# Moving the value products of two mixers to the steps of later heads' scores and transposes

## The chip, the cores and the metric

The kernel runs on one core of one Trainium2 chip. The time is device microseconds of one execution; a run's figure is the median of several executions. TensorE (PE) multiplies, VectorE (DVE) and ScalarE (ACT) work element by element and empty PSUM, GpSimd (POOL) and SyncE (SP) mostly issue transfers. PSUM is the memory of eight banks into which TensorE writes.

## The reference

One block of a streaming encoder, on 256 frames of width 2048, all in float32: a half-step SwiGLU feed-forward, two token mixers side by side, a second feed-forward and a norm. Only the mixers are touched here.

```python
att = chunked_band_attention(q_a, k_a, v_a, rel_bias)      # 8 heads of 128
#   scores = q k^T * 128**-0.5 + bias, masked; p = softmax(scores); out = p v
ret = chunkwise_retention(rotary(q_r), rotary(k_r), v_r)   # 8 heads of 128
#   scores = q k^T * decay; out = scores v; out = out * rsqrt(mean(out * out) + EPS)
ret = silu(g_r) * ret
merged = sigmoid(gate_a) * (att @ w_out_att) + sigmoid(gate_r) * (ret @ w_out_ret)
x = x + merged @ w_out
```

## The kernel before

Nearly all work is matrix products with weights that stream in once. The program is a hand-written list of **steps**. A standard step takes one piece of weights, 256 rows by 512 columns, multiplies it with both halves of the frames and adds into two PSUM banks. For accuracy each float32 number is split into a high part (`hi`, ScalarE, line 126) and a low part (`lo`, VectorE, line 127), and three products of those are added (lines 137, 138 and 140): twelve products of 512 columns in a standard step.

`run` writes the steps out in order. For step c it first prepares weights up to step c+3 (`prep_upto`: a cast on ScalarE and a subtraction on VectorE; four `hi`/`lo` buffers exist, so the cast for step c+3 needs the buffer that step c-1 has read). Then it writes out everything that is due at step c (the table `due`, filled by `later(n, fn)`), and then the products of step c. Each engine does its own instructions in this order, so what is due at step c stands on TensorE ahead of the twelve products of c, and on ScalarE and VectorE behind the split for step c+3.

The mixers' own small products have no steps. They are due at steps of the projections that run meanwhile, and they are plain float32 products, not split ones. Steps are counted here from m, the first step of the second projection of retention's values: m to m+7 is that projection, m+8 to m+23 retention's first queries and keys (heads 0 to 3), m+24 to m+39 its second (heads 4 to 7), m+40 to m+55 the four blocks of attention's output product (`woa`), and from m+56 the four blocks of retention's (`wor`). The second feed-forward comes after them.

Attention, head h, opened at m+4+4h, in stages that the tuple at line 948 places:

- `scores` (tile `as`, +0): two products into a side bank; VectorE then adds the bias and takes the maximum.
- `powers` (+1) and `shares` (+2): exponentials on ScalarE, divisions on VectorE.
- `transposes` (tile `apt`, +4): three transposes into a side bank, which ScalarE copies out (line 937).
- `values` (tile `av`, +6): two products into a side bank; ScalarE casts the result to `atth` (line 376), VectorE subtracts to `attl` (line 377).

So at step m+4+4h stand the transposes of head h-1 and the scores of head h, and two steps later, alone or with a transpose of retention's queries and keys (`qr`, `kr`), the values of head h-1.

Retention, half b (four heads), opened `RET_WAIT[b]` steps after its keys are complete, so at m+37 and m+44: head i has its scores (tile `rs`) at +2i and its values (tiles `ro`) at +2i+3. The four heads of a half share two output banks, and `finish`, at +9, squares them, takes the root on GpSimd and scales them on VectorE into `rg` (line 999). Three steps later `ret.put` transposes `rg` (tile `retp`) and splits it into `reth` and `retl`, which `wor` multiplies. Its block 0 uses heads 4 to 7 from its third step, m+58.

All of `as`, `apt`, `av`, `rs`, `retp`, the transposes of `qr` and `kr`, and `gps` (the turn of a norm's gains, due at m+52, copied out by VectorE at line 293) write **side** tiles, and there are two side banks:

```python
def side_tile(name):
    return psum.tile([P, NB], F32, tag="side", name=name, bufs=2)
```

A tile takes a bank that was given back, and its first product waits until the last reader of that bank is done.

Of the kernel before, what the change touches and what calls it, by code (L numbers as in the profile page):

```python
# [37 lines left out]
HALF_K = D // P // 2  # L38
LEAD = 12
MIX_LEAD = 8  # L40
RET_WAIT = (14, 5)
HELD = 6

SHARE = (0.85,) * 4 + (1.0,) * 4 + (0.8,) + (0.4,) * 3 + (0.15,) * 4
# [28 lines left out]
def block_kernel(ctx: ExitStack, tc: tile.TileContext, x, g1, w1g, w1u, w1d, gm, w_in, rel, woa, wor, wo,  # L73
# [12 lines left out]
    def act_tile(dt, name):  # L86
        return apool.tile([P, 4, SEQ], dt, tag="act", name=name)

    def acc_tile(name, tag="acc"):
        return psum.tile([P, NB], F32, tag=tag, name=name, bufs=3)  # L90

    def side_tile(name):
        return psum.tile([P, NB], F32, tag="side", name=name, bufs=2)

    def tmp_tile(name, tag="t", bufs=None):
        return tmp.tile([P, NB], F32, tag=tag, name=name, bufs=bufs)
# [9 lines left out]
    def later(n, fn):  # L106
        due.setdefault(state["step"] + n, []).append(fn)
# [261 lines left out]
    def rsqrt(dst, ssum, n, width):  # L369

        v = small.tile([P, width], F32, tag="v", name="v")
        nc.vector.tensor_scalar(v, ssum, 1.0 / n, EPS, op0=ALU.mult, op1=ALU.add)
        nc.gpsimd.tensor_tensor(dst, v, mhalf[:, :width], op=ALU.pow)

    def split_out(ps, hi, lo):
        nc.scalar.copy(hi, ps)
        nc.vector.tensor_sub(lo, ps, hi.bitcast(F32))
# [513 lines left out]
    def attention(h):  # L891
        b, i = h // 4, h % 4
        hs = slice(i * HD, (i + 1) * HD)
        sm = {}

        def scores():
            q, k = tposed["qa", b], tposed["ka", b]
            ps = side_tile(f"as{h}")
            nc.tensor.matmul(ps[:, 0:SEQ], q[:, i, P:SEQ], k[:, i, :], start=True, stop=True)
            nc.tensor.matmul(ps[:, SEQ : SEQ + P], q[:, i, 0:P], k[:, i, 0:P], start=True, stop=True)  # L900
            room = act_tile(F32, f"p{h}").rearrange("p a q -> p (a q)")
            s = room[:, : 3 * P].rearrange("p (j k) -> p j k", j=3)
            sm["room"] = room
            p3 = ps[:, : 3 * P].rearrange("p (j k) -> p j k", j=3)

            for j, bj in ((0, 1), (1, 0), (2, 0)):
                nc.vector.scalar_tensor_tensor(
                    s[:, j, :], p3[:, j, :], scale, table["bias", b][:, i, bj * P : (bj + 1) * P], op0=ALU.mult, op1=ALU.add
                )
            m = small.tile([P, NT], F32, tag="m", name="m")  # L910
            tot = small.tile([P, NT], F32, tag="l", name="l")
            for t, js in ((1, slice(0, 2)), (0, slice(2, 3))):
                nc.vector.reduce_max(m[:, t : t + 1], s[:, js, :], axis=AX.XY)
            nc.vector.tensor_scalar_mul(m, m, -1.0)
            sm["p"], sm["m"], sm["tot"] = s, m, tot


        def powers():
            s, m, tot = sm["p"], sm["m"], sm["tot"]
            for t, js in ((1, slice(0, 2)), (0, slice(2, 3))):  # L920
                nc.scalar.activation(
                    s[:, js, :], s[:, js, :], AF.Exp, bias=m[:, t : t + 1], accum_out=tot[:, t : t + 1]
                )

        def shares():
            s, tot = sm["p"], sm["tot"]
            nc.vector.reciprocal(tot, tot)
            for t, js in ((1, slice(0, 2)), (0, slice(2, 3))):
                nc.vector.tensor_scalar_mul(s[:, js, :], s[:, js, :], tot[:, t : t + 1])

        def transposes():
            ps = side_tile(f"apt{h}")

            for j, c in ((2, 0), (0, 1), (1, 2)):
                nc.tensor.transpose(ps[:, c * P : (c + 1) * P], sm["p"][:, j, :], id_sb)
            pt = sm.pop("room")[:, 3 * P : 6 * P]
            nc.scalar.copy(pt, ps[:, : 3 * P])
            sm["pt"] = pt

        def values():  # L940
            v = nat["va", b]
            ps = side_tile(f"av{h}")
            nc.tensor.matmul(ps[:, :SEQ], v[:, 0, hs], sm["pt"][:, :SEQ], start=True, stop=False)
            nc.tensor.matmul(ps[:, P:SEQ], v[:, 1, hs], sm["pt"][:, SEQ:], start=False, stop=True)
            hi, lo = att.alloc(b)
            split_out(ps[:, :SEQ], hi[:, i, :], lo[:, i, :])

        return (0, scores), (1, powers), (2, shares), (4, transposes), (6, values)

    def all_attention():  # L950
        for h in range(HEADS):
            for s, stage in attention(h):
                later(2 + 4 * h + s, stage)

    def retention(b):

        wait = RET_WAIT[b]
        outs = {}

        def head(i):  # L960
            h = 4 * b + i
            hs = slice(i * HD, (i + 1) * HD)
            sm = {}

            def scores():
                q, k = tposed["qr", b], tposed["kr", b]
                ps = side_tile(f"rs{h}")
                nc.tensor.matmul(ps[:, 0:SEQ], k[:, i, 0:P], q[:, i, :], start=True, stop=True)
                nc.tensor.matmul(ps[:, SEQ : SEQ + P], k[:, i, P:SEQ], q[:, i, P:SEQ], start=True, stop=True)
                s = act_tile(F32, f"rp{h}").rearrange("p a q -> p (a q)")[:, : 3 * P]  # L970
                nc.vector.tensor_mul(s[:, :SEQ], ps[:, :SEQ], table["decay", b][:, i, :])
                nc.vector.tensor_mul(s[:, SEQ:], ps[:, SEQ : SEQ + P], table["decay", b][:, i, 0:P])
                sm["s"] = s

            def values():
                if i == 0:
                    for t in range(NT):
                        outs[t] = acc_tile(f"ro{b}{t}", ("acc", "z")[t])
                v = nat["vr", b]
                s = sm["s"]  # L980
                nc.tensor.matmul(outs[0][:, hs], s[:, 0:P], v[:, 0, hs], start=True, stop=True)
                nc.tensor.matmul(outs[1][:, hs], s[:, P:SEQ], v[:, 0, hs], start=True, stop=False)
                nc.tensor.matmul(outs[1][:, hs], s[:, SEQ:], v[:, 1, hs], start=False, stop=True)

            return scores, values

        def finish():
            srcs = []
            for t in range(NT):
                sq = tmp_tile(f"rsq{b}{t}", "gate", 2)  # L990
                nc.scalar.activation(sq, outs[t], AF.Square)
                ms = small.tile([P, 4], F32, tag="ms", name="ms")
                nc.vector.reduce_sum(ms, sq.rearrange("p (h d) -> p h d", h=4), axis=AX.X)
                rs = small.tile([P, 4], F32, tag="rs", name="rs")
                rsqrt(rs, ms, HD, 4)
                o = tmp_tile(f"rg{b}{t}", "qk", 4)
                for i in range(4):
                    hs = slice(i * HD, (i + 1) * HD)
                    nc.vector.scalar_tensor_tensor(
                        o[:, hs], outs[t][:, hs], rs[:, i : i + 1], nat["gr", b][:, t, hs], op0=ALU.mult, op1=ALU.mult  # L1000
                    )
                srcs.append(o)
            later(3, lambda: [ret.put(b, t, srcs[t]) for t in range(NT)])

        for i in range(4):
            for s, stage in enumerate(head(i)):
                later(wait + 2 * i + 3 * s, stage)
        later(wait + 2 * 4 + 1, finish)

    w_in0 = w_in[0]  # L1010

# [37 lines left out]
    for b in range(2):  # L1049
        add([proj(QR + b * NB, ret_qk_done("qr", b)), proj(KR + b * NB, ret_qk_done("kr", b, lambda b=b: retention(b)))])  # L1050
# [207 lines left out]
```

## Time and profile before

| what | before |
|---|---|
| median of 3 runs | 2061.78 us (2060.89 to 2064.99) |
| the profiled execution | 2063.49 us |
| its span, first to last instruction | 2061.4 us |
| TensorE busy | 2045.3 us, 99% of the span |
| VectorE busy | 1754.4 us, 85% |
| ScalarE busy | 1402.9 us, 68% |
| granted TensorE clock, mean | 0.999 of 2.4 GHz |
| HBM read | 462.65 MB |

The profile is of one execution and its times are microseconds from its first instruction. The profiled execution took 2.1 us more than its span and 1.71 us more than the median.

### The profile page before, as it was taken

The numbers are of one execution on the slowest core, as the hardware profiler recorded it, in microseconds if no ns is written. First come the engines' busy times: TensorE is split into PE (matmuls) and PEld (weight loads), VectorE is DVE, ScalarE is ACT, GpSimd is POOL, SyncE is SP. The second block draws the span as 40 slices with busy tenths as digits, with TensorE's granted clock in tenths as the row PEclk, the third lists the DMA queues.
The fourth block names the chain that finished last, engine by engine and source line by source line (L and its number), as shares of the span: only waits on it lengthen the run. The fifth ranks groups of instructions, "written<-read, shape, count | busy, mean of one in ns | idle before, by whom it ended". The sixth has DMA issues, their size and how long they took to land.

```text
span 2061.4 us, 26148 instructions
## 1 busy us (share of the span) xinstructions
PE 2045.3 (99%) x9256; PEld 1691.9 (82%) x9256; DVE 1754.4 (85%) x1824; ACT 1402.9 (68%) x1732; POOL 273.3 (13%) x322
## 2 busy tenths in 40 slices
PE   9999999999999999999999999999999999999998
PEld 7788888888888888888888888888888878888886
DVE  7998899899997799899966667568989988998986
ACT  7677667777777767776665434556776677677785
POOL 1111211122111110122100000010122012110200
PEclk9999999999999999999999999999999999999999
DMA  8776876788678777788775645575787668876873
GB/s 308 207 225 230 269 227 207 239 264 258 191 231 258 240 205 251 258 284 260 227 267 175 223 143 187 187 245 170 235 273 234 200 224 273 240 206 233 281 215 133
DMA packets 219315, 473.28 MB, mean 230 GB/s; under 512 B 14816, under 2 KB 15568, under 8 KB 219184
## 3 DMA queue, kind: packets, MB, share of 16 engines
q1 hardware_dynamic: 161088, 309.89, 44.7%
q0 software_dynamic: 54752, 155.88, 27.9%
q10 hardware_dynamic: 3344, 5.84, 0.8%
q8 instruction: 72, 1.18, 0.2%
q14 instruction: 59, 0.48, 0.1%
HBM read 462.65 MB, written 8.91 MB: 229 GB/s over the span
## 4 chain that ended last, share of the span: by engine, by line
PE 93%; DVE 3%; DMA 2%; ACT 1%; issue 1%; SPq 0%; DVEq 0%; POOLq 0%; POOL 0%; ACTq 0%
PE acc L140 17%; PE acc L137 17%; PE acc L138 17%; DMA raw<-in_ffn_w_down_dram 2%; DVE lo L127 1%; ACT hi L126 0%; PE z684a L140 0%; PE z380a L137 0%; PE z953a L138 0%; PE z684a L138 0%; PE z418a L137 0%; PE z723a L138 0%; PE z380a L140 0%; PE z281a L138 0%; PE z723a L137 0%
## 5 line engine op out<-in xcount | busy, mean ns | idle before, releaser
L127 DVE TENSOR_TENSOR lo<-raw,hi 128x1024 fp32r<-128x1024 f32 x399 | 487.1, 1224 | 179.1 <-ACT hi L126 174.3
L126 ACT CAST hi<-raw 128x1024 fp32r<-128x1024 f32 x399 | 417.7, 1050 | 226.8 <-PE acc L138 143.7
L775 ACT ACTIVATE acc<-xall 128x512 f32<-128x512 f32 x96 | 57.5, 599 | 8.0 <-DVE f1g L742 3.6
L778 ACT ACTIVATE xall<-acc 128x512 f32<-128x512 f32 x96 | 56.6, 589 | 9.2 <-PE acc L140 7.4
L137 PE MATMUL acc<-hi,mgh 128*128 128x512 f32 x128 | 50.2, 392 | 0.0
L138 PE MATMUL acc<-hi,mgl 128*128 128x512 f32 x128 | 49.9, 390 | 0.0
L137 PE MATMUL acc<-hi,nma01h 128*128 128x512 f32 x96 | 38.7, 403 | 0.0
L137 PE MATMUL acc<-hi,nma00h 128*128 128x512 f32 x96 | 38.6, 402 | 0.0
L138 PE MATMUL acc<-hi,nma00l 128*128 128x512 f32 x96 | 37.5, 391 | 0.0
L137 PE MATMUL acc<-hi,nma10h 128*128 128x512 f32 x96 | 37.5, 391 | 0.0
L138 PE MATMUL acc<-hi,nma01l 128*128 128x512 f32 x96 | 37.5, 390 | 0.0
L138 PE MATMUL acc<-hi,nma11l 128*128 128x512 f32 x96 | 37.5, 390 | 0.0
L137 PE MATMUL acc<-hi,nma11h 128*128 128x512 f32 x96 | 37.4, 390 | 0.0
L138 PE MATMUL acc<-hi,nma10l 128*128 128x512 f32 x96 | 37.4, 390 | 0.0
L140 PE MATMUL acc<-lo,mgh 128*128 128x512 f32 x128 | 35.6, 390 | 0.0
L140 PE MATMUL acc<-lo,nma01h 128*128 128x512 f32 x96 | 29.6, 390 | 0.0
L140 PE MATMUL acc<-lo,nma00h 128*128 128x512 f32 x96 | 29.6, 390 | 0.0
L140 PE MATMUL acc<-lo,nma11h 128*128 128x512 f32 x96 | 29.6, 390 | 0.0
L140 PE MATMUL acc<-lo,nma10h 128*128 128x512 f32 x96 | 29.6, 390 | 0.0
L140 PEld LDWEIGHTS acc<-lo,mgh 128*128 128x128 f32 x128 | 24.0, 188 | 5.0
L137 PEld LDWEIGHTS acc<-hi,mgh 128*128 128x128 f32 x128 | 24.1, 188 | 4.9
L138 PEld LDWEIGHTS acc<-hi,mgl 128*128 128x128 f32 x128 | 24.1, 188 | 4.8
(6130 smaller groups left out, 6933.7 us busy)
## 6 DMA issues: line engine op xcount, KB each, us to landing
raw<-in_ffn_w_down_dram SPq DMA_DIRECT2D x176, 512.0 KB, 6.1
raw<-in_w_in_dram SPq DMA_DIRECT2D x96, 512.0 KB, 4.7
raw<-in_ffn_w_up_dram SPq DMA_DIRECT2D x32, 512.0 KB, 10.2
raw<-in_w_out_dram SPq DMA_DIRECT2D x32, 512.0 KB, 4.0
raw<-in_ffn_w_gate_dram SPq DMA_DIRECT2D x31, 512.0 KB, 5.9
raw<-in_w_out_att_dram SPq DMA_DIRECT2D x16, 512.0 KB, 4.3
raw<-in_w_out_ret_dram SPq DMA_DIRECT2D x16, 512.0 KB, 4.0
z380x<-in_w_in_dram POOLq DMA_DIRECT2D x8, 512.0 KB, 7.4
```

The source lines that it names most:

```text
L126: nc.scalar.copy(hi, raw)
L127: nc.vector.tensor_sub(lo, raw, hi.bitcast(F32))
L137: nc.tensor.matmul(acc, ahi, whi, start=first, stop=False, **more)
L138: nc.tensor.matmul(acc, alo, whi, start=False, stop=False, **more)
L140: nc.tensor.matmul(acc, ahi, wlo, start=False, stop=last, **more)
L775: nc.scalar.activation(acc, xs[t][:, cols], AF.Copy, scale=2.0)
L778: nc.scalar.activation(xs[t][:, cols], acc, AF.Copy, scale=0.5)
```

## The change

Three numbers move. Attention's values are due eight steps after their scores in place of six, so that values of h-2, transposes of h-1 and scores of h now share a step, in this order. Retention's values are due four steps after their scores in place of three, which makes them share a step with the scores of head i+2. Its first half opens two steps later, and `finish` comes one step later relative to its half.

```diff
-RET_WAIT = (14, 5)
+RET_WAIT = (16, 5)
...
-        return (0, scores), (1, powers), (2, shares), (4, transposes), (6, values)
+        return (0, scores), (1, powers), (2, shares), (4, transposes), (8, values)
...
             for s, stage in enumerate(head(i)):
-                later(wait + 2 * i + 3 * s, stage)
-        later(wait + 2 * 4 + 1, finish)
+                later(wait + 2 * i + 4 * s, stage)
+        later(wait + 2 * 4 + 2, finish)
```

In steps:

| what | before | after |
|---|---|---|
| attention, scores of h / transposes of h | m+4+4h / m+8+4h | the same |
| attention, values of h | m+10+4h | m+12+4h |
| retention, scores of heads 0 to 3 | m+37, 39, 41, 43 | m+39, 41, 43, 45 |
| retention, values of heads 0 to 3 | m+40, 42, 44, 46 | m+43, 45, 47, 49 |
| retention, finish / put of the first half | m+46 / m+49 | m+49 / m+52 |
| retention, scores of heads 4 to 7 | m+44, 46, 48, 50 | the same |
| retention, values of heads 4 to 7 | m+47, 49, 51, 53 | m+48, 50, 52, 54 |
| retention, finish / put of the second half | m+53 / m+56 | m+54 / m+57 |

The order in which TensorE stands to do its work around step m+16, as a difference (- before, + after). `av1` is the value product of head 1, `apt2` the transposes of head 2, `as3` the scores of head 3; a bracket names the engine's counter on which the instruction waits.

```order
-L943 MATMUL av1_9328<-p1_9178,va0_8071 128x256 [waits Activation_49]
-L944 MATMUL av1_9328<-p1_9178,va0_8071 128x128
...
+L943 MATMUL av1_9376<-p1_9178,va0_8071 128x256 [waits DVE_49]
+L944 MATMUL av1_9376<-p1_9178,va0_8071 128x128
 L935 MATMUL apt2_9381<-id_sb_78,p2_9281 128x128 [waits DVE_49,PE_49]
 L935 MATMUL apt2_9381<-id_sb_78,p2_9281 128x128 x2
-L899 MATMUL as3_9386<-ka0T_7123,qa0T_6271 128x256 [waits PE_49]
+L899 MATMUL as3_9386<-ka0T_7123,qa0T_6271 128x256 [waits Activation_49]
 L900 MATMUL as3_9386<-ka0T_7123,qa0T_6271 128x128
```

The two products of `av1` went down two steps, to just ahead of `apt2`, and the scores `as3` behind them now wait on ScalarE's counter, where before they waited on TensorE's own.

ScalarE at the same place, before. `hi` are casts of weights, `qr00` and `qr01` empty the two banks of retention's query projection (line 869), `p2<-apt2` copies the transposes out.

```order
L376 CAST atth0_9230<-av1_9328 128x256 [waits PE_49]
L126 CAST hi586_9348<-raw586_9225 128x1024 [waits DMAHW6_49,PE_49,Activation_49]
L869 ACTIVATE qr00_9366<-acc64_0_9187,nmrstd_91 128x512 [waits PE_49]
L869 ACTIVATE qr01_9368<-acc64_1_9188,nmrstd_91 128x512 [waits PE_49]
L126 CAST hi587_9371<-raw587_9253 128x1024 [waits DMAHW7_49,Activation_49]
L937 COPY p2_9281<-apt2_9381 128x384 [waits PE_49]
```

And after:

```order
L126 CAST hi586_9343<-raw586_9225 128x1024 [waits DMAHW6_49,PE_49,Activation_49]
L869 ACTIVATE qr00_9361<-acc64_0_9187,nmrstd_91 128x512 [waits PE_49]
L869 ACTIVATE qr01_9363<-acc64_1_9188,nmrstd_91 128x512 [waits PE_49]
L126 CAST hi587_9366<-raw587_9246 128x1024 [waits DMAHW7_49,Activation_49]
L376 CAST atth0_9269<-av1_9376 128x256 [waits PE_49]
L937 COPY p2_9281<-apt2_9381 128x384 [waits PE_49]
```

The cast `atth` of the value product moved from ahead of `hi586` to between `hi587` and the copy of `apt2`.

TensorE at step m+52, before: the values of head 6 at m+51 (`ro`, from `rp6`), the gains' turn `gps2` at m+52, the values of head 7 at m+53.

```order
L981 MATMUL ro10_10323<-vr1_9161,rp6_10351 128x128
L982 MATMUL ro11_10324<-vr1_9161,rp6_10351 128x128
L983 MATMUL ro11_10324<-vr1_9161,rp6_10351 128x128
...
L292 MATMUL gps2_10458<-id_sb_78,grows2_10217 128x16 [waits DMASW7_49,DVE_49]
...
L981 MATMUL ro10_10323<-vr1_9161,rp7_10414 128x128 [waits DVE_49]
```

And after, where `retp00` and `retp01` are the transposes of retention's first half:

```order
L981 MATMUL ro10_10314<-vr1_9161,rp6_10322 128x128 [waits DVE_49]
L982 MATMUL ro11_10315<-vr1_9161,rp6_10322 128x128
L983 MATMUL ro11_10315<-vr1_9161,rp6_10322 128x128 [waits DVE_49]
L292 MATMUL gps2_10442<-id_sb_78,grows2_10208 128x16 [waits DMASW7_49]
L382 MATMUL retp00_10447<-id_sb_78,rg00_10356 128x128 [waits DVE_49]
L382 MATMUL retp00_10447<-id_sb_78,rg00_10356 128x128 x3
L382 MATMUL retp01_10454<-id_sb_78,rg01_10369 128x128 [waits DVE_49]
L382 MATMUL retp01_10454<-id_sb_78,rg01_10369 128x128 x3
```

The values of head 6 and both transposes of the first half came to the step of `gps2`: three side tiles in one step, of which the third, `retp01`, waits on VectorE. The rows of VectorE at that place, after, from the end of `finish` of the first half to the split of its first transposes:

```order
L999 SCALAR_TENSOR_TENSOR rg01_10369<-ro01_10172,rs_10365,gr0_9372 128x128 x3
L127 TENSOR_TENSOR lo621_10387<-raw621_10238,hi621_10386 128x1024 [waits DMAHW1_49,PE_49,Activation_49]
L971 TENSOR_TENSOR rp7_10398<-rs7_10395,decay1_9507 128x256 [waits PE_49]
L972 TENSOR_TENSOR rp7_10398<-rs7_10395,decay1_9507 128x128
L127 TENSOR_TENSOR lo622_10414<-raw622_10265,hi622_10413 128x1024 [waits DMAHW2_49,PE_49,Activation_49]
L1072 TENSOR_TENSOR siga2_10078<-acc70_0_10325,siga2_10078 128x512 [waits DMASW5_49,PE_49]
L1072 TENSOR_TENSOR siga2_10078<-acc70_1_10326,siga2_10078 128x512 [waits PE_49]
L127 TENSOR_TENSOR lo623_10434<-raw623_10289,hi623_10433 128x1024 [waits DMAHW3_49,Activation_49]
L293 COPY gains_79<-gps2_10442 128x16 [waits PE_49]
L377 TENSOR_TENSOR retl0_10446<-retp00_10447,reth0_10445 128x4x128 [waits Activation_49]
```

The copy `gains` that frees the bank for `retp01` stands behind three splits, a decay product and two evictions; before, `finish` of the first half was three steps further away.

## Rows read from the trace of the kernel before

**Rows 1.** The page's first part: busy us, share of span, instructions.

```profile
PE 2045.3 (99%) x9256; PEld 1691.9 (82%) x9256; DVE 1754.4 (85%) x1824; ACT 1402.9 (68%) x1732; POOL 273.3 (13%) x322
```

**Rows 2.** Waits of PE, 1050 to 1300 us: total us, times, longest.

```profile
PE kr0p L382 <- DVE attl L377: 0.6, 1, 0.6
```

**Rows 3.** Timeline of PE: start us, length us, what. Visits at m+14, m+18, m+19.

```profile
1090.29 0.59 PE L943 MATMUL av<-p,va 128*128 128x256 f32 x2
...
1091.18 0.39 PE L138 MATMUL acc<-hi,nma01l 128*128 128x512 f32 x1
...
1102.89 0.59 PE L943 MATMUL av<-p,va 128*128 128x256 f32 x2
...
1103.54 0.60 PE L382 MATMUL qr0p<-id_sb,qr00r 128*128 128x128 f32 x4
...
1104.21 0.40 PE L138 MATMUL acc<-hi,nma01l 128*128 128x512 f32 x1
...
1106.74 0.60 PE L382 MATMUL qr0p<-id_sb,qr01r 128*128 128x128 f32 x4
...
1107.41 0.40 PE L138 MATMUL acc<-hi,nma01l 128*128 128x512 f32 x1
```

**Rows 4.** Timeline of PE, step m+16 and step m+20.

```profile
1096.42 0.49 PE L935 MATMUL apt<-id_sb,p 128*128 128x128 f32 x3
1096.74 0.60 PE L899 MATMUL as<-ka0T,qa0T 128*128 128x256 f32 x2
...
1109.95 0.49 PE L935 MATMUL apt<-id_sb,p 128*128 128x128 f32 x3
```

**Rows 5.** Timeline of ACT at steps m+16, m+18 and m+20.

```profile
1097.20 1.04 ACT L126 CAST hi<-raw 128x1024 fp32r<-128x1024 f32 x1
1098.14 0.48 ACT L937 COPY p<-apt 128x384 f32<-128x384 f32 x1
...
1103.74 0.37 ACT L376 CAST atth<-av 128x256 fp32r<-128x256 f32 x1 [0.46 <-PE av L944]
1104.17 0.59 ACT L828 COPY qr0T<-qr0p 128x512 f32<-128x512 f32 x1
...
1109.28 1.05 ACT L126 CAST hi<-raw 128x1024 fp32r<-128x1024 f32 x1 [2.15 <-PE acc L138]
1110.48 0.48 ACT L937 COPY p<-apt 128x384 f32<-128x384 f32 x1 [0.15 <-PE apt L935]
```

**Rows 6.** The one wait of Rows 2: timeline of DVE.

```profile
1133.13 0.42 DVE L377 TENSOR_TENSOR attl<-av,atth 128x256 fp32r<-128x256 f32 x1
```

**Rows 7.** The same wait: timeline of PE, idle time and releaser in brackets.

```profile
1133.61 0.66 PE L382 MATMUL kr0p<-id_sb,kr01r 128*128 128x128 f32 x4 [0.59 <-DVE attl L377]
```

**Rows 8.** Timeline of PE at m+52, m+53 and m+56.

```profile
1220.05 0.23 PE L292 MATMUL gps<-id_sb,grows 16*128 16x16 f32 x1
1220.21 0.50 PE L137 MATMUL acc<-hi,atth 128*128 128x512 f32 x1
...
1223.11 0.38 PE L981 MATMUL ro<-vr,rp 128*128 128x128 f32 x2
...
1232.78 0.48 PE L137 MATMUL acc<-hi,reth 128*128 128x512 f32 x1
```

**Rows 9.** Timeline of DVE, m+50 to m+57.

```profile
1214.64 0.42 DVE L971 TENSOR_TENSOR rp<-rs,decay 128x256 f32<-128x256 f32 x1
...
1221.93 0.17 DVE L293 COPY gains<-gps 128x16 f32<-128x16 f32 x1
...
1231.17 2.36 DVE L127 TENSOR_TENSOR lo<-raw,hi 128x1024 fp32r<-128x1024 f32 x2
...
1235.76 1.29 DVE L377 TENSOR_TENSOR retl<-retp,reth 128x512 fp32r<-128x512 f32 x2
```

**Rows 10.** Timeline of PE: one of its longest waits, in the second feed-forward.

```profile
1663.20 0.50 PE L137 MATMUL acc<-hi,f2a1h 128*128 128x512 f32 x1 [1.17 <-ACT hi L126]
```

**Rows 11.** Windows: stretch, length, busy us by engine, PEclk, DMA share, GB/s.

```profile
1600.00:1700.00 100.00, 98.77 (x447) 81.47 (x446) 92.41 (x88) 70.73 (x82) 10.73 (x12) 1.00 0.67 208
```

## Prediction, made before the changed kernel was run

> **What bounds the kernel.** I read the page's first part, then TensorE's waits around the mixers, then the timelines of TensorE, ScalarE and VectorE there. TensorE is busy 99% of the span [rows 1], and between 1050 and 1300 us, where all moved work lies, it waits once, 0.59 us [rows 2, 7]. So TensorE's queue sets the end: what the change takes from it or adds to it as waiting comes out of the total, and nothing that it saves on another engine does. From the second product of step m+14 (1091.18) to the first transpose of m+16 (1096.42) lie 23 intervals of 0.228 us [rows 3, 4], so a standard step takes 2.73 us.
>
> **What joining visits saves.** The change adds and removes no instruction; it lets float32 visits between the split products fall together. A visit of `av` alone takes 0.89 us from its start to the second standard product (1090.29 to 1091.18), a visit of four transposes alone 0.67 (1106.74 to 1107.41), and a joined one of both 1.32 (1102.89 to 1104.21) [rows 3]. Each figure holds one interval of 0.228, so two visits apart cost 0.89 + 0.67 - 0.23 = 1.33 and joined 1.32. By the change's step table the visits go from 36 to 30, since several values leave steps that they already shared with transposes of `qr` and `kr`. Six joins at 0.01 save 0.06 us.
>
> One wait goes: the second transpose of retention's first keys, `kr0p`, waited 0.59 us for the `attl` of a value product one step before it [rows 6, 7]. That value product now comes two steps later, so 0.6 us is gained.
>
> **What the new order makes wait, attention.** Three side tiles now stand in one step on two side banks: values of h-2, transposes of h-1, scores of h. The third needs a bank that one of the two before it in the same step must give back. The order rows show which: the scores wait on ScalarE's counter, and the last ScalarE work ahead that reads such a bank is the copy of the transposes, line 937. Before, every bank that scores took was long free. This holds for heads 2 to 7, six times; behind the scores TensorE's whole queue stands.
>
> Let T be the start of the step's visit. Without a wait the transposes begin at T + 0.65, as behind `av` at 1102.89 and 1103.54 [rows 3], and the scores 0.32 later [rows 4], at T + 0.97. The copy is later. ScalarE first does the cast for step c+3, then `atth`, then the copy.
>
> - *Heads 2, 4 and 6* (m+12, 20, 28). The cast ends at T + 0.38 (1109.28 + 1.05 against 1109.95) [rows 4, 5]. `atth` starts 0.85 after the value product does (1103.74 against 1102.89) and the next ScalarE work 0.43 after that [rows 3, 5]; so the copy runs from T + 1.28 for 0.48, to T + 1.76. TensorE goes on 0.06 after a release (1133.13 + 0.42 against 1133.61) [rows 6, 7]. The scores start at T + 1.82, a wait of 0.85.
> - *Heads 3, 5 and 7* (m+16, 24, 32). A projection has just ended, and ScalarE empties its banks before it casts. The copy stands at T + 1.72 already (1098.14 against 1096.42) behind a cast of 1097.20 [rows 4, 5]. Now `atth` takes that place and the copy follows 0.43 later, from T + 2.15 to T + 2.63. The scores start at T + 2.69, a wait of 1.72.
>
> Together 3 x 0.85 + 3 x 1.72 = 7.7 us. No row of before shows this wait. It is least if ScalarE had `atth` out of the way for nothing: then the copy starts 0.53 after the transposes do (1110.48 against 1109.95) [rows 4, 5], at T + 1.18, or at T + 1.72, and the waits are 0.75 and 1.29, together 6.1. I take 7.7, since the order rows put `atth` ahead of the copy.
>
> **Retention.** Its scores and values meet in steps with at most two side tiles, one bank was read long before, and I find no wait there. Two places of `put` are tighter.
>
> - *Step m+52.* `gps2`, `retp00` and `retp01` are three side tiles, and `retp01` waits for the copy `gains` on VectorE. Counted from the start S of step m+49, where `finish` of the first half begins: the same `finish`, after the same single `ro` visit, began at 1223.11 and let VectorE on to the next split at 1231.17, S + 8.06 [rows 8, 9]. Behind it stand three splits, two evictions and a decay product. The first five took 1231.17 to 1235.76, 4.59 us, and the decay product is some 0.6 (0.42 for the larger of its two) [rows 9]. So `gains` starts at S + 13.2 and, at 0.17, releases at S + 13.4. TensorE gets to `retp01` after three steps, a visit of `ro`, one of `ro` and `rs` (0.66 each, as `av` less its interval), a third `ro`, `gps2` (0.16) and four transposes (0.36): 8.19 + 2.64 + 0.52 = S + 11.4 [rows 3, 8]. The wait is 2.0. If VectorE were not behind, `gains` would end about 2.05 after the start of `gps2` as it does before (1220.05, 1222.10), and `retp01`, which TensorE reaches 0.6 + 0.16 + 0.36 after the place where `gps2` stood, would still wait 0.9 [rows 8, 9]. I take 2.0: the order rows show the queue.
> - *Step m+58.* The second half's `put` comes at m+57, its reader at m+58: one step between in place of two. `retl` starts at 1235.76, 12.65 after 1223.11, and its first half is done about 0.65 later, 13.3 [rows 8, 9]; VectorE's work in between is the same in number and kind. TensorE's product of step m+56 began 9.67 after 1223.11 [rows 8]; that is now step m+57, and the second product of m+58 comes 2.73 + 0.23 later, at 12.6. Before there was one more step, 15.4, and no wait. Now 0.7.
>
> **Transfers.** No transfer moves in any queue. Tiles of scores are given back by value products two steps later at most, 5.5 us, and the loads of the merge's gates take such tiles. They are due eleven steps before VectorE reads them, 30 us, which I let hide this. A load that came late would hold VectorE's queue, and with it the split of the next weights, for what is missing, at most those 5.5 us.
>
> **Sum.** 7.7 + 2.0 + 0.7 - 0.6 - 0.1 = 9.7 us on a profiled time of 2063.49, which is its span of 2061.4 and 2.1 around it: 2073.2. That execution lies 1.71 above the median of the runs, so I forecast 2061.78 + 9.7 = **2071.5**, 0.47% slower. What would have to make up for it is idle time behind the mixers, and in 250 us there is none; later waits are for transfers, which start when buffers come free and so move along with TensorE.
>
> A rule that prices waits higher: the Trainium skill, "TensorE: Matmul & The Clock Gate", section "Single matmul latency", gives a matmul a fixed part of 398 cycles at 2.4 GHz, 0.166 us, which an uninterrupted stream hides and each wait could expose. By that estimate eight waits would add 1.3 us and the sum be 11.0. The row at 1133.61 shows TensorE going on 0.06 us after the release [rows 6, 7], which is in the waits above; its idle time of 0.59 agrees with no such part.
>
> **Rivals.**
> 1. *No wait, 2061.1.* If the scores found a free bank in time, only the gains would be left, 0.66 us: no change. For it the copy has to land by T + 0.91, 0.85 or 1.72 us earlier than worked out. The cast of ScalarE alone ends at T + 0.38, and `atth` cannot start before T + 0.85, so only another bank would do it, and the order rows name ScalarE. 9 in 100.
> 2. *Joining pays after all, under 2057.7.* Six joins would have to be worth 0.6 us each to make the kernel faster by over 0.2%. The joined visit measured 0.01 [rows 3]. 3 in 100.
> 3. *The clock falls.* If after each of the seven longest waits one step ran at 1.2 GHz, 7 x 2.73 = 19 us would come on top: 2091. Against it: a wait of 1.17 us lies in a stretch whose granted clock is 1.00, that is 2.4 GHz [rows 10, 11]; waits of 1.7 and 2.0 are not in the trace. 4 in 100. The same page of the Trainium skill, section "Why this matters for your kernels", warns that gaps in TensorE's work can bring the clock back to its lower level.
> 4. *The forecast*, waits of this kind and about this size: 84 in 100.
>
> **Range.** Least, attention's 6.1 and nothing in retention, less 0.7: +5.4, or 2067.2; runs scatter by 1 below, so 2066. Most, if the casts come as late at heads 2, 4 and 6 as at the others, 6 x 1.72 in place of 7.7: +12.3, or 2074.1, and runs scatter upwards too: 2076. That holds case 4, 84 in 100. A difference of 0.2%, 4.1 us, is about what a measurement of this kernel can tell from none: slower by more than that in cases 3 and 4, 0.88; within it in case 1, 0.09; faster in case 2, 0.03.
>
> **What would show it.** In the changed profile TensorE's waits name the copy `p` of line 937 as releaser of `as`, six times, three near 0.85 and three near 1.7; `gains` as releaser of `retp`, once; `retl` for a product of `wor`, once; `kr0p` no longer waits. Behind each wait the granted clock stays at 1.00. TensorE's busy time is unchanged. It is wrong if the scores wait less than 0.3 us each, if the second feed-forward swallows the delay, or if joined visits prove shorter than their parts by tenths of a microsecond.

## The result, and the profile after

The changed kernel took 2072.67 us (median of 6 runs, 2070.43 to 2074.16); the kernel before, run beside it, 2062.74 (6 runs, 2060.89 to 2065.55). The ratio is 1.0046, 95% interval 1.0034 to 1.0058: slower, where 2071.5 had been forecast. The profiled executions have spans of 2072.0 and 2061.4 us, 10.6 apart.

The page's first part of the changed kernel; the counts are those of [rows 1], and TensorE is 3.8 us busier. Forecast was no change; 2.9 of it is not the program's, since a second execution of the changed kernel (below) shows 2046.2:

```profile
PE 2049.1 (99%) x9256; PEld 1695.4 (82%) x9256; DVE 1755.6 (85%) x1824; ACT 1402.9 (68%) x1732; POOL 273.8 (13%) x322
```

The waits of TensorE from 1050 to 1300 us, where [rows 2] had one:

```profile
PE as L899 <- ACT p L937: 5.9, 6, 1.4
PE retp L382 <- DVE gains L293: 1.6, 1, 1.6
```

Six waits of scores on the copy of p, one of the transposes on the gains, and `kr0p` gone. This view counts idle time from the end that the profile models for the product ahead, so it shows less than a wait costs and leaves the shortest out. The same view of TensorE's weight loads (PEld), each of which stands ahead of its product, has a third entry, a product of `wor` that waits for `retl`:

```profile
PEld as L899 <- ACT p L937: 7.3, 6, 1.6
PEld retp L382 <- DVE gains L293: 1.9, 1, 1.9
PEld acc L138 <- DVE retl L377: 0.5, 1, 0.5
```

How one of the three short waits comes about (step m+12), first TensorE's timeline, then ScalarE's:

```profile
1084.42 0.59 PE L943 MATMUL av<-p,va 128*128 128x256 f32 x2
...
1085.07 0.49 PE L935 MATMUL apt<-id_sb,p 128*128 128x128 f32 x3
1086.13 0.70 PE L899 MATMUL as<-ka0T,qa0T 128*128 128x256 f32 x2 [0.57 <-ACT p L937]
1086.67 0.38 PE L900 MATMUL as<-ka0T,qa0T 128*128 128x128 f32 x2
```

```profile
1083.76 1.05 ACT L126 CAST hi<-raw 128x1024 fp32r<-128x1024 f32 x1 [1.67 <-PE acc L138]
1085.27 0.37 ACT L376 CAST atth<-av 128x256 fp32r<-128x256 f32 x1 [0.47 <-PE av L944]
1085.60 0.48 ACT L937 COPY p<-apt 128x384 f32<-128x384 f32 x1
```

The copy ends at 1086.08 and the scores begin 0.05 us later, 1.71 after the visit's start. The cast was out of the way long before; `atth`, which can start only when the value product is done, is what holds the copy. At step m+16 (heads 1, 2 and 3) the cast of the weights holds it as well:

```profile
1097.81 0.59 PE L943 MATMUL av<-p,va 128*128 128x256 f32 x2
...
1100.34 0.70 PE L899 MATMUL as<-ka0T,qa0T 128*128 128x256 f32 x2 [1.39 <-ACT p L937]
```

```profile
1098.60 1.04 ACT L126 CAST hi<-raw 128x1024 fp32r<-128x1024 f32 x1
1099.53 0.38 ACT L376 CAST atth<-av 128x256 fp32r<-128x256 f32 x1
1099.80 0.49 ACT L937 COPY p<-apt 128x384 f32<-128x384 f32 x1
```

These answer to [rows 4, 5], where the same scores came 0.32 us behind their transposes. The seventh wait is at step m+52, TensorE and then VectorE:

```profile
1226.54 0.23 PE L292 MATMUL gps<-id_sb,grows 16*128 16x16 f32 x1
1226.70 0.66 PE L382 MATMUL retp<-id_sb,rg 128*128 128x128 f32 x4
1228.98 1.07 PE L382 MATMUL retp<-id_sb,rg 128*128 128x128 f32 x4 [1.63 <-DVE gains L293]
1229.71 0.78 PE L137 MATMUL acc<-hi,atth 128*128 128x512 f32 x1
1230.28 0.63 PE L138 MATMUL acc<-hi,attl 128*128 128x512 f32 x1
1230.71 0.63 PE L137 MATMUL acc<-hi,atth 128*128 128x512 f32 x1
```

```profile
1227.63 1.22 DVE L127 TENSOR_TENSOR lo<-raw,hi 128x1024 fp32r<-128x1024 f32 x1
1228.77 0.17 DVE L293 COPY gains<-gps 128x16 f32<-128x16 f32 x1
```

`gps` was ready at 1226.77, but VectorE came to its copy only at 1228.77, behind its queue. What follows the wait was not forecast: four transposes take 1.07 us where the ones before them took 0.66, and products come 0.43 apart, not 0.23. The windows (length, busy us of PE, PEld, DVE, ACT and POOL, granted clock, DMA share, GB/s) say why:

```profile
1226.00:1228.00 2.00, 1.36 (x11) 0.97 (x9) 2.00 (x4) 1.16 (x2) 0.00 (x0) 1.00 0.81 262
1228.00:1230.00 2.00, 1.01 (x5) 1.02 (x6) 1.53 (x3) 0.00 (x0) 0.00 (x0) 0.77 0.80 207
1230.00:1232.00 2.00, 2.00 (x7) 1.52 (x6) 0.69 (x1) 0.59 (x1) 0.00 (x0) 0.50 0.79 222
1232.00:1234.00 2.00, 2.00 (x9) 1.66 (x8) 0.00 (x0) 0.42 (x1) 0.00 (x0) 0.88 0.23 88
1234.00:1236.00 2.00, 2.00 (x10) 1.65 (x10) 1.23 (x1) 0.79 (x2) 0.00 (x0) 1.00 0.00 0
```

The clock fell to its lower level, 1.2 GHz, behind the idle time, and was back at 1.00 from 1234 us on. Behind the waits of 1.39 us in attention it stayed at 1.00.

### The profile page after: what moved, and what is told of

Read it like the earlier page. It is cut to its first block, busy times and chain, and to the rows that moved or that the text cites. A ratio compares the mean times of both kernels' runs of the same rounds, so it can differ in the third digit from the quotient of the medians.

```text
span 2072.0 us, 26146 instructions
## 1 busy us (share of the span) xinstructions
PE 2049.1 (99%) x9256; PEld 1695.4 (82%) x9256; DVE 1755.6 (85%) x1824; ACT 1402.9 (68%) x1732; POOL 273.8 (13%) x322
## 4 chain that ended last, share of the span: by engine, by line
PE 93%; DMA 2%; DVE 2%; ACT 1%; issue 1%; DVEq 0%; POOLq 0%; POOL 0%; ACTq 0%
PE acc L140 17%; PE acc L137 17%; PE acc L138 17%; DMA raw<-in_ffn_w_down_dram 2%; DVE lo L127 1%; DMA raw<-in_w_in_dram 1%; ACT hi L126 0%; PE z684a L140 0%; PE z243a L140 0%; PE z684a L137 0%; PE z380a L140 0%; PE z953a L137 0%; PE z281a L138 0%; PE z205a L137 0%; PE z51a L137 0%
## 5 line engine op out<-in xcount | busy, mean ns | idle before, releaser
L126 ACT CAST hi<-raw 128x1024 fp32r<-128x1024 f32 x399 | 417.6, 1050 | 238.9 <-PE acc L138 153.1
```

Source lines behind the costliest of these rows:

```text
L126: nc.scalar.copy(hi, raw)
```

## Experiments

The theory: the third side tile of a step waits for a bank that is emptied in the same step, and the wait ends when the engine that empties it comes to that work in its queue. The rivals: the values' or retention's lateness costs by itself; joined visits pay and are hidden under the waits; the clock is most of it. Each kernel was timed beside the kernel before; where a kernel is named "the changed kernel" the other edits stand. The table adds a length that is free of what happens elsewhere in the program: from the first score product of head 0 to the first transposes of the second norm (`n2p`), in the profiled execution, less the 244.80 us of the kernel before.

| kernel | runs | median us | ratio to before [95%] | stretch, us over before | clock fell |
|---|---|---|---|---|---|
| changed | 6 | 2072.67 | 1.0046 [1.0034, 1.0058] | +9.81 | yes |
| attention only | 5 | 2071.24 | 1.0037 [1.0024, 1.0050] | +6.42 | no |
| retention only | 10 | 2065.48 | 1.0014 [1.0005, 1.0024] | +1.87 | no |
| values at +7 | 10 | 2066.00 | 1.0014 [1.0005, 1.0023] | +3.02 | yes |
| scores in other banks | 10 | 2063.98 | 1.0006 [0.9997, 1.0016] | +0.91 | no |
| gains a step later | 6 | 2069.67 | 1.0033 [1.0020, 1.0045] | +6.50 | no |
| both cures | 10 | 2062.36 | 0.9997 [0.9988, 1.0007] | -0.98 | no |
| values last | 6 | 2070.31 | 1.0037 [1.0025, 1.0049] | +7.12 | yes |
| copy on VectorE | 4 | 2076.66 | 1.0065 [1.0049, 1.0082] | +15.24 | twice |
| gains 13 times | 4 | 2075.45 | 1.0061 [1.0046, 1.0076] | +13.10 | yes |
| changed, again | 5 | 2070.81 | 1.0037 [1.0024, 1.0050] | +8.31 | no |

**One part of the change alone.** Attention's values moved, retention as before:

```diff
-RET_WAIT = (16, 5)
+RET_WAIT = (14, 5)
...
-                later(wait + 2 * i + 4 * s, stage)
-        later(wait + 2 * 4 + 2, finish)
+                later(wait + 2 * i + 3 * s, stage)
+        later(wait + 2 * 4 + 1, finish)
```

> Only the eight value products of the attention heads move two steps later; the retention steps stand where they stood before. Theory (the third side tile of a step waits for a bank that is emptied in the same step): the six waits of the score products on ScalarE's copy of p come, about 0.6 us three times and 1.4 us three times, 2.5 us of lateness for each pair of heads; the wait on the gains stays away and with it the stretch at 1.2 GHz. Six visits of 0.84 and 1.66 us in turn make +7.5, less 0.7 for the wait of kr0p that goes: 6.8 us above the kernel before, ratio 1.0033, 3.8 below the changed kernel. Rival A (the later retention is what costs): within 1 us of the kernel before. Rival B (the stretch at the lower clock and the wait on the gains are most of it): under 3 us above before.

Measured +6.42 us in the stretch, forecast +6.8, and the only waits there are attention's six:

```profile
PE as L899 <- ACT p L937: 5.9, 6, 1.4
```

Retention moved, attention's values as before:

```diff
-        return (0, scores), (1, powers), (2, shares), (4, transposes), (8, values)
+        return (0, scores), (1, powers), (2, shares), (4, transposes), (6, values)
```

> Only the retention steps move; the value products of attention stand where they stood before. Theory: the wait of the third tile of step m+52 on the gains comes alone, 1.6 us on TensorE's row and 1.9 us of lateness, then 1.6 us for products at 1.2 GHz if the clock falls here too, and 0.3 us for the low parts at m+58: 3.8 us above before, ratio 1.0018, and no wait of a score product on the copy of p. If the clock stays at 1.00 behind the same wait, 2.2 us above before. Rival A (the later retention is most of the cost): 7 us or more above before.

Measured +1.87, where 2.2 had been forecast for a clock that stays; it stayed, behind the same wait:

```profile
1222.00 0.66 PE L382 MATMUL retp<-id_sb,rg 128*128 128x128 f32 x4 [1.63 <-DVE gains L293]
```

The two parts add up, 6.42 + 1.87 = 8.29 against 8.31 of the changed kernel in its execution without the clock's fall. So attention's waits are three quarters of the loss, and neither the later retention nor the clock is most of it. The stretch is of one execution each. The medians are coarser: over the kernel before beside them, 8.2 us for attention's part and 2.4 for retention's, and for the changed kernel 9.9 in its first measurement and 7.8 in the second.

**The third tile, taken away in two ways.** Values one step later than before instead of two, so that they have a visit of their own:

```diff
-        return (0, scores), (1, powers), (2, shares), (4, transposes), (8, values)
+        return (0, scores), (1, powers), (2, shares), (4, transposes), (7, values)
```

> As the changed kernel, but the value products of attention stand one step later than before instead of two: later than before all the same, in a visit of their own, with no transposes and no scores of a following head in the step. Theory: no step of attention holds three side tiles, so the six waits on the copy of p are gone, and the visits of values cost what they cost before: 7.5 us below the changed kernel (ratio to before 1.0015), the wait on the gains and the stretch at 1.2 GHz remaining. Rival C (the values' lateness, the longer life of p and v, costs): less than 4 us below the changed kernel. Rival D (the joined visits save something that the waits hide): less than 7.5 us below it, by what the joins are worth.

And the steps as the change has them, the scores in an accumulator bank:

```diff
-            ps = side_tile(f"as{h}")
+            ps = acc_tile(f"as{h}")
```

> As the changed kernel, with every step where it is, but the score tile of a head is taken from the three banks of the accumulators instead of the two side banks. Theory: the scores no longer wait for the bank that the copy of p empties; the six waits go and the visits are still joined: 7.5 us below the changed kernel (ratio to before 1.0015), a little more if joins pay (rival D: 1 to 2 us more). If the accumulators' ring is itself short by then, waits of acc tiles on their evictions come instead, and less than 7 us comes back. Rival C (lateness of values itself): no more than 2 us below the changed kernel.

All six waits are gone in both; the stretch is 6.8 us shorter than the changed kernel's in the first and 8.9 in the second, where 7.5 had been forecast for both; the medians' differences are 6.7 and 8.7. The first had the clock's fall as the changed kernel did; the second did not, so 1.5 of its 8.9 is that (below), and 7.4 the waits. In the second the scores follow their transposes at once, in the same joined visit:

```profile
1097.36 0.49 PE L935 MATMUL apt<-id_sb,p 128*128 128x128 f32 x3
1097.69 0.60 PE L899 MATMUL as<-ka0T,qa0T 128*128 128x256 f32 x2
1098.12 0.39 PE L900 MATMUL as<-ka0T,qa0T 128*128 128x128 f32 x2
```

So values that come two steps late cost nothing by themselves. The first gives back 0.6 us less than the second, clock aside, and is 0.64 longer already from the first score product to the first product of `woa` (115.47 and 114.83). Half of that comes from the transposes `qr00`, `kr00` and `qr10`, whose visits take 0.1 us longer each there; the rest may be what the second's joins are worth. The rows also show a small part of each wait that is not idle time: the pair of score products takes 0.54 us to the next start behind a wait (1086.13 to 1086.67) and 0.43 here.

**The order within a step.** Scores ahead of values:

```diff
-        for h in range(HEADS):
-            for s, stage in attention(h):
+        heads = [attention(h) for h in range(HEADS)]
+        for n in (3, 0, 1, 2, 4):
+            for h in range(HEADS):
+                s, stage = heads[h][n]
```

> As the changed kernel, but in a step the order is transposes, scores, values instead of scores of later heads behind values. The third side tile of a step is then the values' tile, which waits for the bank of the transposes' tile, emptied by the same copy of p, while the scores' visit fills part of that time. Theory: the three short waits shrink to about 0.1 us and the three long ones to about 1 us, since ScalarE's cast still stands ahead of the copy: 3 us below the changed kernel. Rival G (each step of three tiles costs the same in any order): within 1 us of the changed kernel.

The stretch is 2.69 us shorter than the changed kernel's (3 forecast), both with the clock's fall. In attention now the values wait, and only where scores of heads 3, 5 and 7 stand:

```profile
PE av L943 <- ACT p L937: 3.3, 3, 1.1
```

**The engine that empties the bank.** The copy of p moved from ScalarE to VectorE:

```diff
-            nc.scalar.copy(pt, ps[:, : 3 * P])
+            nc.vector.tensor_copy(pt, ps[:, : 3 * P])
```

> As the changed kernel, but the copy of p out of the transposes' bank is made by VectorE instead of ScalarE. Theory (the wait of the score tile lasts as long as the queue of the engine that empties the bank): on VectorE the copy stands behind the low part of the inputs (1.23 us) and the low part of the values (attl), which itself waits for ScalarE's high part. By the changed kernel's rows the copy would start 0.7 us later in steps of even heads (1086.31 in place of 1085.60) and 1.3 us later in those of odd ones (1101.14 in place of 1099.80): three waits of about 1.3 us and three of about 2.7 us, 6.2 us above the changed kernel; if the granted clock falls behind the three long waits, as it did behind 1.6 us on the gains, up to 5 us more. Rival H (the wait is the bank's own turn-round, whoever empties it, or ScalarE's cast alone): within 1 us of the changed kernel, or faster, since ScalarE's cast no longer stands ahead.

Slower, as the theory said, but by shorter waits than forecast: three of 0.89 us and three of 2.32. TensorE's row of step m+16, and VectorE's:

```profile
1099.72 1.04 PE L899 MATMUL as<-ka0T,qa0T 128*128 128x256 f32 x2 [2.32 <-DVE attl L377]
```

```profile
1098.10 1.23 DVE L127 TENSOR_TENSOR lo<-raw,hi 128x1024 fp32r<-128x1024 f32 x1 [2.74 <-ACT hi L126]
1099.25 0.42 DVE L377 TENSOR_TENSOR attl<-av,atth 128x256 fp32r<-128x256 f32 x1
1099.58 0.55 DVE L937 COPY p<-apt 128x384 f32<-128x384 f32 x1
```

The scores began 0.05 us behind the end of `attl` (1099.67) and ahead of the copy's (1100.13): here they stand in the values' bank, not in the transposes'. Which of the two banks the third tile gets is settled when the program is built, and moving the copy changed it; the forecast had taken the bank for fixed. The rule itself held, the wait ends with the last reader of the bank, in the order of that reader's queue. The scores now start 2.03 and 3.47 us after the visit's start instead of 1.71 and 2.53, so 3 x 0.32 + 3 x 0.94 = 3.8 us; the stretch is 6.93 longer than that of the changed kernel's second execution, and neither fell behind the gains. The other 3.1 goes with two falls of the clock, behind the first and the third of the long waits (near 1100 and 1161 us) and not behind the second (near 1131):

```profile
1100.00:1102.00 2.00, 2.00 (x7) 1.62 (x7) 0.90 (x5) 0.00 (x0) 0.00 (x0) 0.50 0.67 196
...
1132.00:1134.00 2.00, 2.00 (x11) 1.64 (x10) 1.89 (x8) 0.00 (x0) 0.00 (x0) 1.00 0.76 243
...
1162.00:1164.00 2.00, 2.00 (x6) 1.55 (x6) 1.83 (x8) 0.00 (x0) 1.06 (x2) 0.50 0.76 245
```

**The wait on the gains.** Their turn one step later, so that step m+52 holds two side tiles:

```diff
-    at(merges[0][0] + 4, lambda: later(8, load_gain(g2, 2)))
+    at(merges[0][0] + 4, lambda: later(9, load_gain(g2, 2)))
```

> As the changed kernel, but the gains of the second merge (gps) are made one step later, so that the step m+52 holds two side tiles and not three. Theory: the wait of retp on the gains, 1.6 us on TensorE's row and 1.9 us of lateness, goes, and with it the stretch at a granted clock of 0.5 behind it, 1.6 us: 3.5 us below the changed kernel. Rival E (the lower clock came by itself at that place and not by the wait): only 1.9 us below, and the granted clock still falls between 1228 and 1234 us. Rival F (VectorE's queue is late there whatever the step): the wait moves to the next side tile, and under 1 us comes back.

The stretch is 3.31 us shorter than the changed kernel's (3.5 forecast), the median 3.0; the wait is gone and the clock stays at 1.00. That it stays proves nothing about the cure, since it also stayed behind this wait in other executions. Against the changed kernel's second execution the stretch is 1.81 shorter. VectorE is as late as before, but nobody waits for it:

```profile
1232.15 0.17 DVE L293 COPY gains<-gps 128x16 f32<-128x16 f32 x1
```

This edit and the scores' other bank together:

> The two cures together: score tiles from the accumulators' banks, gains of the second merge one step later; the moved steps stay where the changed kernel has them, so all joined visits stay. Theory: all seven waits and the lower clock go; what is left of the change is kr0p's wait gone (0.7 us less) and joins that are worth nothing: 0 to 1 us below before, ratio 0.9995 to 1.0000, which is within what a measurement tells. Rival D (joins pay): 2 us or more below before, ratio under 0.999. Rival C (later values cost by themselves): 2 us or more above before.

The view of the products' waits lists none from 1050 to 1300 us, and the time is that of the kernel before, 0.9997 of it, with an interval on both sides of 1. So the seven waits and what follows them are the whole loss. That the stretch is 0.98 us shorter than before is one execution each; the medians, 2062.36 and 2063.07, can't be told apart. This is the fastest version found, and no measurable gain over the kernel before.

**When the clock falls.** The wait on the gains made longer, by copying them 13 times:

```diff
-            nc.vector.tensor_copy(gains[:, i, :], ps[:, : D // P])
+            for _ in range(13 if i == 2 else 1):
+                nc.vector.tensor_copy(gains[:, i, :], ps[:, : D // P])
```

> As the changed kernel, but VectorE copies the gains of the second merge 13 times in place of once, so that the one wait on the gains is some 1.0 us longer (12 small copies at about 0.08 us): 2.6 us in place of 1.6. The clock fell behind this wait of 1.6 us in three of the five profiles that hold it, and in none behind the waits of 1.4 us. Theory I (the idle time's length counts, and 1.6 us is at the edge): the granted clock falls to 0.5 behind the wait, 1.3 to 2 us of lateness; in all 1.0 above the changed kernel's profiled execution. Rival J (the fall hangs on something else at that place): the clock may stay at 1.00 behind the longer wait, and the span is 0.6 below the changed kernel's.

And the changed kernel once more:

> The changed kernel as it is, for one more look at the same wait on the same chip as the two others: does the clock fall again behind the 1.63 us on the gains? If the fall is fixed by the program, yes, between 1228 and 1233 us and for about 1.6 us of lateness; if it is a matter of chance at this length, the profile may show 1.00 there and a span about 1.6 us shorter.

The 13 copies took 2.66 us, 0.2 each and not 0.08, so the wait was 4.1 us and not 2.6. The clock fell while it still lasted:

```profile
1226.00:1228.00 2.00, 0.13 (x2) 0.00 (x0) 1.93 (x5) 0.59 (x1) 0.00 (x0) 1.00 0.64 209
1228.00:1230.00 2.00, 0.00 (x0) 0.00 (x0) 1.68 (x10) 0.00 (x0) 0.00 (x0) 0.58 0.80 244
1230.00:1232.00 2.00, 1.75 (x6) 1.58 (x7) 0.77 (x2) 0.59 (x1) 0.00 (x0) 0.50 0.44 171
```

In the second execution of the changed kernel it did not fall, behind the same wait:

```profile
1227.94 0.66 PE L382 MATMUL retp<-id_sb,rg 128*128 128x128 f32 x4 [1.62 <-DVE gains L293]
```

```profile
1228.00:1230.00 2.00, 2.00 (x11) 1.74 (x12) 1.17 (x2) 0.59 (x1) 0.00 (x0) 1.00 0.70 231
```

The two executions of one program differ by 1.51 us in the stretch (254.61 and 253.11): that is the price of this fall. The 4.1 us wait made the stretch 4.79 longer than in the second, 2.5 of it the longer wait and 2.3 the fall. So it is not fixed by the program, and it came more often behind longer idle time, and the one behind 4.1 us cost more; what else decides stays open.

## Why the prediction was right, point by point

**What bounds the kernel** held: every wait that was added to TensorE's queue is in the total, every one that was taken away came back. The price of the first rival was wrong, though: with the scores in a free bank, retention's 2.0 and 0.7 stay, so it is 2.0 us above the kernel before and not 0.7 below it; the kernel with the scores in other banks came out 0.9 above.

**Attention, 7.7 us; measured 7.5.** From its first product to the standard one behind it the joined visit takes 2.39 us at heads 2, 4 and 6 and 3.21 at heads 3, 5 and 7, and 1.55 at all six in the kernel with both cures: 3 x 0.84 + 3 x 1.66. The forecast was 0.85 and 1.72. Behind that agreement two small errors cancel. The scores started at T + 1.71 and T + 2.53, not T + 1.82 and T + 2.69, since the copy followed `atth` after 0.33 and 0.27 us and not after 0.43. And a wait costs 0.1 us more than the shift of the scores' start (from T + 0.98), in all 0.27 more than the idle time of its row (0.57 and 1.39). The Trainium skill, "TensorE: Matmul & The Clock Gate", section "Single matmul latency", gives a single matmul a fixed part of 0.166 us, from which the prediction estimated what a wait could expose. The score products lose 0.1 us, 0.6 over the six waits; that this is the same part no run shows.

**Gains, 2.0 us; measured 1.9.** `retp01` was due 0.36 behind 1226.70 and started at 1228.98. The reason was that given, VectorE's queue.

**`retl` at m+58, 0.7 us; measured 0.3.** The second product came 0.45 us after the first and the third 0.34 after that, against 0.23 between others:

```profile
1249.05 0.39 PE L137 MATMUL acc<-hi,reth 128*128 128x512 f32 x1
1249.50 0.50 PE L138 MATMUL acc<-hi,retl 128*128 128x512 f32 x1
1249.84 0.39 PE L137 MATMUL acc<-hi,reth 128*128 128x512 f32 x1
```

The mechanism was right and the size off. The view of the products' waits does not list it; that of the weight loads does, and the spacing shows it.

**`kr0p`, 0.6 us gained; measured 0.8.** That wait is gone in every kernel that has attention's values moved. The 0.59 of its row is idle time, not its price. In the kernel before, `qr01r` started 0.45 us after the products listed ahead of it (1106.74 [rows 3]), and `kr0p` 1.20 after them (1133.61 [rows 7]); from there to the second standard product it took 0.73 and not 0.67:

```profile
1106.29 0.62 PE L140 MATMUL acc<-lo,nma11h 128*128 128x512 f32 x2
...
1132.41 0.61 PE L140 MATMUL acc<-lo,nma11h 128*128 128x512 f32 x2
...
1134.34 0.39 PE L138 MATMUL acc<-hi,nma01l 128*128 128x512 f32 x1
```

One gain like it was overlooked. In the kernel before, the eight transposes of retention's first `put` held 0.35 us of waiting inside one row; behind both cures they take 1.04 (first the kernel before, then both cures):

```profile
1209.16 1.38 PE L382 MATMUL retp<-id_sb,rg 128*128 128x128 f32 x8
```

```profile
1218.36 1.04 PE L382 MATMUL retp<-id_sb,rg 128*128 128x128 f32 x8
```

It was a side tile's bank again: the weights of the fifth transpose, the first of `retp01`, waited for a decay product (line 972) that reads such a bank. The view of the weight loads' waits names it in the kernel before, where [rows 2], of the products alone, does not:

```profile
PEld retp L382 <- DVE rp L972: 0.4, 1, 0.4
```

**Joins, 0.06 us.** 7.5 + 1.9 + 0.3 - 0.8 - 0.35 + 1.5 of clock is 10.05, and the stretch grew by 9.81; without the clock it is 8.55 against 8.31. The 0.2 left over may be the joins; that it is was not shown.

**The clock** is the step that failed: "Behind each wait the granted clock stays at 1.00", argued from a wait of 1.17 us [rows 10, 11]. It held for six of the seven waits, and at the seventh, the longest, it failed in this execution and held in another of the same program. The rival had 19 us for seven falls; one fall, at one wait, cost 1.5.

**The sum** was 9.7, the spans differ by 10.6 and the medians by 9.9. The clock's 1.5 was missing; the overlooked 0.35, the smaller `retl`, the larger `kr0p` and the remainder make up for it within the stretch. So that the total came so close is partly luck: without the clock's fall the stretch grew by 8.31, and the medians of the second measurement lie 7.8 apart. The stretch holds 9.81 of the 10.6. The rest lies outside the moved work: the first score product came 1.28 us later than in the kernel before, and what follows the stretch was 0.5 shorter; why is not shown.

## What to carry to other kernels

Count the tiles that one step takes from a ring of banks: where it takes more than there are banks, the engine that fills them waits for one that empties them, as long as that engine's queue has other work in front. The queue's order sets the price (0.84 us behind one cast, 1.66 behind two), and a bank from another ring or one step's delay for one tile takes all of it away. Joining small visits on a saturated TensorE was worth next to nothing, so it was no ground to accept any wait. Ask for the waits of the weight loads as well as those of the products: they named two (0.35 and 0.3 us here) that the products' list leaves out. And take a wait's price from the shift of what stands behind it, not from its idle time.

## What the runs showed of the hardware

The granted clock can fall behind a single short idle time of TensorE, and does not each time: behind 1.38 to 1.39 us in none of 15 waits (five profiles), behind 1.62 to 1.63 in three of seven profiles, behind 2.32 in two of three waits, behind 4.1 in the one there was. Before all of them TensorE had been busy without a break for the step ahead. The Trainium skill, "TensorE: Matmul & The Clock Gate", section "Why this matters for your kernels", warns that gaps in TensorE's work can bring the lower level back; these runs agree that they can, with 1.5 us lost to one gap of 1.63, which is shorter than those that the page warns of.

A score product behind a wait takes 0.1 us longer to its successor than one that follows others (0.54 against 0.43), beside the 0.05 us from the release to its start.
